# Where TensorE's weights and streamed operands lie against each other in SBUF

## The chip, the cores and the metric

The kernel runs on one core of one Trainium2 chip. The metric is the device time of one execution in microseconds (us). Three runs of the kernel before took 1624.79, 1626.24 and 1630.22 us; their median is 1626.24 us. In this text "place" is an offset along the free dimension of SBUF, the same in all 128 partitions, and "pace" is the time from the start of one matmul to the start of the next.

## The reference

Two models run one after the other on 256 tokens of width 1024, in float32. The first has two layers of: a gated feed-forward, a mixer with three branches (neighbourhood attention, gated linear attention, latent attention), and another gated feed-forward. The second has two hybrid layers and a final norm. Cut to what carries the work:

```python
def swiglu(h, w1, w3, w2):
    return (jax.nn.silu(h @ w1) * (h @ w3)) @ w2
...
    for l in range(DEPTH):                      # first model, 2 layers
        x = x + 0.5 * swiglu(rms_norm(x, ffn1_norm[l]), ffn1_w1[l], ffn1_w3[l], ffn1_w2[l])
        h = rms_norm(x, mix_norm[l])
        z = h @ w_in[l]                         # 1024 x 6752
        ...                                     # three branches on parts of z
        mixed = (gt[:, :, 0] * (y_na @ w_br_na[l])
                 + gt[:, :, 1] * (y_gla @ w_br_gla[l])
                 + gt[:, :, 2] * (y_mla @ w_br_mla[l]))
        x = x + mixed @ w_out[l]
        x = x + 0.5 * swiglu(rms_norm(x, ffn2_norm[l]), ffn2_w1[l], ffn2_w3[l], ffn2_w2[l])
...
    for l in range(DEPTH):                      # second model, 2 hybrid layers
        x = hybrid_layer(x, ...)                # x @ w_in, attention, convolution, mixed @ w_out
    return rms_norm_2(x, final_g)
```

The feed-forward width is 2816. Nearly all of the arithmetic is products of 256 tokens with weight matrices that are read once from HBM.

## The kernel before

The activations lie transposed, features on the partitions and 256 tokens along the free dimension. Every weight matrix is cut into slabs of 128 partitions by up to 1024 columns. The list of slabs is written in `emit` (`ffn_slabs`, `group`, `G`, `B`, `A`, lines 1711 to 1762), and the kernel takes them in that order.

One slab goes through three steps. `fetch` (L311) starts its DMA on SyncE's queue into one of five `raw` tiles. `convert` (L326) splits it into two float32r tiles: ScalarE writes the rounded part `H` (L337), VectorE writes the rest `L` = raw - H (L341). There are three `H` and three `L` buffers. `take` (called from `col`, `group` and others) hands the pair to TensorE and starts the fetch and conversion of a later slab. The activations are split in the same way into a high and a low part (`xh`, `xl`; `gh`, `gl` in the feed-forward; `yh`, `yl` and `mh`, `ml` in the mixers), so that each product is three matmuls: high by high, high by low, low by high.

Slabs are used in two ways.

- Loaded as weights (`mm3`, L430 to 433, called from `col`, `out_proj` and the second half of `ffn`): 128 columns of `H` or `L` are loaded into the array, and 256 tokens of the activation stream past. Three matmuls for each 128 columns, 24 for a full slab. L431 loads `H` and streams the high activations, L432 loads `H` and streams the low ones, L433 loads `L` and streams the high ones. All four feed-forwards work in this way: 44 slabs of 24 matmuls and 24 slabs of 21 or 24 each, 1584 matmuls; 6336 in the four.
- Streamed (`group`, L506 to 508, and L855 to 857 for the latent attention's second projection): 128 tokens of the activation are loaded as weights, and up to 512 columns of `H` or `L` stream past.

While one matmul streams, the weights of the next are loaded: the profile has LDWEIGHTS on a line of its own (PEld) beside the matmuls (PE).

Where a slab lies in its buffer comes from the table `PLACES`. A buffer is 1024 + 120 columns long, and slab number n uses the pair `PLACES[n % 320]`, the first for `H`, the second for `L`, in columns of 4 bytes. In the built program the streamed activations (`xh`, `xl`, `gh`, `gl`, `yh`, `yl`, `mh`, `ml`) begin 128 bytes past a multiple of 512, and every 256-token part of them too. The three `H` buffers begin 320, 288 and 256 bytes past a multiple of 512, the three `L` buffers 224, 192 and 160. So the distance of a loaded slab from the operand that streams past it, taken modulo 512 bytes, is worked out from its number; the buffers are used in the order first, third, second. In this kernel that distance differs from slab to slab.

The vector engines' work for the branches, the norms and the gates is spread over `tick` calls between matmuls.

Of the kernel before, what the change touches and what calls it, by code (L numbers as in the profile page):

```python
# [10 lines left out]
F32R = mybir.dt.float32r  # L11
# [6 lines left out]
P = 128  # L18
# [5 lines left out]
W2CUT = ((0, 7), (7, 7), (14, 8))  # L24
EPS = 1e-6
NEG = -1e30
SKEW = 120


def places():  # L30

    c = [[(16 * ((5 * i + 3 * j) % 8), 16 * j) for j in range(8)] for i in range(8)]
    c = [c[i][(j + i) % 8] for j in range(8) for i in range(8)]
    f = [(8 * a, 8 * b) for a in range(16) for b in range(16) if a % 2 or b % 2]
    return c + [f[(i * 77) % len(f)] for i in range(len(f))] + c[::-1]


PLACES = places()
BIG = 3e38
UNITS = "a0 a1 a2 a3 f0 b0 f1 b1 b2 b3".split()  # L40

# [3 lines left out]
class Pack:  # L45
# [5 lines left out]
    def add(self, name, a):  # L51
        a = np.asarray(a, np.float32).reshape(P, -1)
        self.at[name] = (self.n, self.n + a.shape[1])
        self.parts.append(a)
        self.n += a.shape[1]
# [78 lines left out]
def lay(I):  # L134
    I = {k: np.asarray(v) for k, v in I.items()}
    A = {}
    A["x"] = I["x"][0].T.reshape(KD, P, T).transpose(1, 0, 2)
    f13, f2 = [], []
    for l in range(2):
        for f in ("ffn1", "ffn2"):  # L140
# [3 lines left out]
            f2.append(w.transpose(2, 1, 0, 3).reshape(KD, P, FF))  # L144
    A["f13"], A["f2"] = np.stack(f13), np.stack(f2)

# [15 lines left out]
    for l in range(2):  # L162
# [36 lines left out]
        rpb.append(tz.transpose(1, 0, 2))  # L199
    A["mA"], A["mM"], A["uq"], A["ukv"] = np.stack(mA), np.stack(mM), np.stack(uq), np.stack(ukv)  # L200
    A["mG"], A["mB"], A["mO"], A["p1"] = np.stack(mG), np.stack(mB), np.stack(mO), np.stack(p1)
    A["up"], A["rpb"] = np.stack(up), np.stack(rpb)
    A["_p1"] = p.at
# [65 lines left out]
class Kernel:  # L269
# [41 lines left out]
    def fetch(s, between=(None,)):  # L311

        if s.pos == len(s.slabs):
            return
        src, cols, gain = s.slabs[s.pos]
        s.pos += 1
        raw = s.wp.tile([P, 1024], F32, tag="raw", name="raw", bufs=5)
        w = cols // len(between)
        for j, f in enumerate(between):
            a = slice(j * w, (j + 1) * w)  # L320
            s.nc.sync.dma_start(raw[:, a], src[:, a])
            if f:
                f()
        s.loaded.append((raw, cols, gain))

    def convert(s, n=1):  # L326

        if not s.loaded:
            return
        raw, cols, gain = s.loaded.pop(0)  # L330
        H, L = (s.wp.tile([P, 1024 + SKEW], F32R, tag=n, name=n, bufs=3)[:, o:o + 1024] for n, o in zip("HL", PLACES[s.nslab % len(PLACES)]))
        s.nslab += 1
        gs = gain() if gain else [None] * n
        w = cols // len(gs)

        def high(g, a):
            s.A.activation(H[:, a], raw[:, a], AF.Copy, **({} if g is None else {"scale": g}))  # L337

        def low(g, a):
            if g is None:  # L340
                s.V.tensor_tensor(L[:, a], raw[:, a], H[:, a].bitcast(F32), OP.subtract)  # L341
            else:
                s.V.scalar_tensor_tensor(L[:, a], raw[:, a], g, H[:, a].bitcast(F32), OP.mult, OP.subtract)

        parts = [(g, slice(j * w, (j + 1) * w)) for j, g in enumerate(gs)]
        if n > 1:
            s.todo += [lambda f=f, p=p: f(*p) for p in parts for f in (high, low)]
        else:
            s.todo += [lambda f=f: [f(*p) for p in parts] for f in (high, low)]
        s.ready.append((H, L))  # L350
# [1308 lines left out]
def setup(s):  # L1659
    nc, i = s.nc, s.i  # L1660
    s.xT = s.C("xT", [P, KD, T])
    s.xh, s.xl = s.C("xh", [P, KD, T], F32R), s.C("xl", [P, KD, T], F32R)
    s.ident = s.C("ident", [P, P])
    make_identity(nc, s.ident)
    s.ones = s.C("ones", [P, P])
    nc.gpsimd.memset(s.ones, 1.0)
    s.one = s.ones[:, :1]
    s.mhalf = s.C("mhalf", [P, 16])
    nc.gpsimd.memset(s.mhalf, -0.5)
    s.A.activation(s.W("ms", [P, 2]), s.mhalf[:, :2], AF.Silu)  # L1670
# [19 lines left out]
def setup_2(s):  # L1690

    s.ypad, s.hTd = cut(s.zero[:, :572], 2), s.zero[:, 572:].rearrange("p (c g h n) -> p c g h n", c=2, g=2, h=4)
    s.nc.gpsimd.memset(s.zero, 0.0)


def emit(tc, i, out, names):
    with ExitStack() as es:
        es.enter_context(tc.manual_schedule())
        s = Kernel(es, tc, i, names)
        prm = [[None, None], [None, None]]  # L1700

        def col(b, l, n):
            a, e = names["_p%d" % (b + 1)][n]
            return prm[b][l][:, a:e]

        def load(b, l, q=s.nc.gpsimd):
            n = "p%d" % (b + 1)
            prm[b][l] = s.W("prm", [P, max(i["p1"].shape[2], i["p2"].shape[2])])[:, :i[n].shape[2]]
            q.dma_start(prm[b][l], i[n][l])

        slabs = []
        add = lambda src, cols, gain=None: slabs.append((src, cols, gain))

        def ffn_slabs(j):
            for f in range(2 * NF):
                add(i["f13"][j, f], 1024)
            for m in range(KD):
                for k, n in W2CUT:
                    add(i["f2"][j, m][:, k * P:(k + n) * P], n * P)

        for l in range(2):
            ffn_slabs(2 * l)
            group = lambda g: [add(i["mA"][l, g, h], 1024) for h in range(4)]
            gain = lambda n, l=l: (lambda: [col(0, l, n)[:, k:k + 1] for k in range(2)])
            group(0)
            add(i["mM"][l], 1024)
            group(3)
            add(i["uq"][l][:, :512], 512, gain("cq"))
            add(i["uq"][l][:, 512:], 1024, gain("cq"))
            for k in range(2):  # L1730
                add(i["ukv"][l][:, k * 1024:(k + 1) * 1024], 1024, gain("ckv"))
            for g in (1, 4, 2, 5, 6):
                group(g)
            for b in range(3):
                G = lambda h: [add(i["mG"][l, (2, 0, 1)[b], 4 * h + j], 1024) for j in range(4)]
                for h in range(2):
                    G(h)
                    for j in range(2):
                        add(i["mB"][l, b, 2 * h + j], 1024, (lambda: [s.hg]) if b == 2 else None)
            for h in range(2):  # L1740
                for j in range(4):
                    add(i["mO"][l, h, j], 1024)
            ffn_slabs(2 * l + 1)
        for l in range(2):
            B = lambda a, b: [add(i["hB"][l, j], 1024) for j in range(a, b)]
            B(6, 10)
            B(0, 2)
            for j in range(4):
                add(i["hA4"][l, j], 568)
            A = lambda g: [add(i["hA"][l, g, j], 1024) for j in range(4)]  # L1750
            A(1)
            B(2, 6)
            B(12, 14)
            A(0)
            B(10, 12)
            B(14, 16)
            B(16, 18)
            add(i["pw"][l], 512)
            for h in range(2):
                for j in range(4):  # L1760
                    add(i["hO"][l, h, j], 1024)
        s.stream(slabs)

        setup(s)
        s.start(lambda: col(0, 0, "g_ffn1"), lambda: load(0, 0, s.nc.sync))
        late = setup_late(s)
        next(late)
        s.spawn(late, 8)
        for l in range(2):
            s.p1 = lambda n: col(0, l, n)  # L1770
            s.hg = s.W("hg", [P, 1])
            s.V.tensor_scalar(s.hg, s.p1("gla"), 0.5, None, OP.mult)
            s.ffn(lambda m: s.xn(m, s.p1("g_mix")), *((6, False) if l == 0 else ()))
            s.mix(l, lambda m: s.xn(m, s.p1("g_ffn2")))
            nb, nl = (0, 1) if l == 0 else (1, 0)
            if nb:
                setup_2(s)
            load(nb, nl)
            s.ffn(lambda m: s.xn(m, col(nb, nl, "g" if nb else "g_ffn1")))
        for l in range(2):  # L1780
            s.p2 = lambda n: col(1, l, n)
            if l == 0:
                load(1, 1)
            s.hybrid(l, (lambda m: s.xn(m, col(1, 1, "g"))) if l == 0 else s.last)
        s.final(out)
# [24 lines left out]
```

## Time and profile before

| | us |
|---|---|
| median of three runs | 1626.24 |
| lowest, highest | 1624.79, 1630.22 |
| the profiled execution | 1627.97 |
| its span, first to last instruction | 1626.2 |
| PE busy | 1598.5 (98%) |
| PEld busy | 1494.1 (92%) |
| DVE busy | 1115.1 (69%) |
| ACT busy | 863.2 (53%) |
[...]

PE is TensorE's matmuls, PEld its weight loads, DVE is VectorE, ACT is ScalarE. [...] The pace is read from the starts.

### The profile page before, as it was taken

How to read it: one execution, taken by the hardware profiler on the slowest of the kernel's cores; microseconds unless marked ns; L12 is line 12 of the kernel's file. 1: busy time of each engine (PE TensorE's matmuls, PEld its weight loads, DVE VectorE, ACT ScalarE, POOL GpSimd, SP SyncE). 2: the span in 40 equal slices, each digit the busy share in tenths (PEclk: the TensorE clock that was granted, in tenths of full speed). 3: DMA queues.
4: the chain of work that ended last, by engine and by line, in shares of the span. 5: the costliest groups of instructions: out<-in, count | busy, mean ns of one | idle time of the engine just before them, and what ended most of it. 6: DMA issues, size and time to landing. Idle time of an engine off the chain costs nothing.

```text
span 1626.2 us, 30862 instructions
## 1 busy us (share of the span) xinstructions
PE 1598.5 (98%) x12446; PEld 1494.1 (92%) x12446; DVE 1115.1 (69%) x1841; ACT 863.2 (53%) x1455; POOL 246.6 (15%) x334
## 2 busy tenths in 40 slices
PE   8999999999999999999999999999999999998998
PEld 8999988799999999999998879999999988887887
DVE  6666667667676665666656776777666578868885
ACT  5444466654445444444446765444444435864684
POOL 2000232311030001100013231103000221113101
PEclk9999999999999999999999999999999999999999
DMA  6555554433555556655565453455555655336431
GB/s 246 189 184 178 195 189 143 163 113 136 185 172 182 188 177 189 197 183 180 179 201 174 143 168 117 143 183 171 193 182 181 191 193 203 114 113 212 172 111 53
DMA packets 78127, 275.92 MB, mean 170 GB/s; under 512 B 8768, under 2 KB 8912, under 8 KB 77984
## 3 DMA queue, kind: packets, MB, share of 16 engines
q1 hardware_dynamic: 76320, 267.47, 48.9%
q0 software_dynamic: 1520, 6.22, 1.2%
q8 instruction: 97, 1.59, 0.4%
q14 instruction: 46, 0.38, 0.1%
q10 hardware_dynamic: 144, 0.26, 0.0%
HBM read 272.87 MB, written 1.05 MB: 168 GB/s over the span
## 4 chain that ended last, share of the span: by engine, by line
PE 92%; DVE 3%; POOL 2%; ACT 1%; issue 1%; DMA 1%; SPq 0%; POOLq 0%; DVEq 0%; ACTq 0%
PE pd L431 21%; PE pd L433 21%; PE pd L432 21%; PE pd L506 4%; PE pd L507 4%; PE pd L508 4%; PE pa L432 2%; PE pa L431 2%; PE pa L433 2%; PE pa L699 2%; PE pa L448 1%; POOL ss L466 1%; DVE L L341 1%; DVE xl L455 1%; PE pa L678 1%
## 5 line engine op out<-in xcount | busy, mean ns | idle before, releaser
L341 DVE TENSOR_TENSOR L<-raw,H 128x1024 fp32r<-128x1024 f32 (+2 forms) x490 | 593.8, 1217 | 241.2 <-ACT H L337 238.5
L337 ACT ACTIVATE H<-raw 128x1024 fp32r<-128x1024 f32 (+2 forms) x490 | 503.3, 1029 | 300.8 <-PE pd L432 115.0
L431 PE MATMUL pd<-xh,H 128*128 128x256 f32 x1840 | 523.1, 284 | 0.0
L433 PE MATMUL pd<-xh,L 128*128 128x256 f32 x1840 | 517.2, 281 | 0.8 <-DVE L L341 0.8
L432 PE MATMUL pd<-xl,H 128*128 128x256 f32 x1840 | 517.2, 281 | 0.3 <-DVE xl L455 0.2
L431 PEld LDWEIGHTS pd<-xh,H 128*128 128x128 f32 x1840 | 347.3, 189 | 7.2 <-issue 6.4
L432 PEld LDWEIGHTS pd<-xl,H 128*128 128x128 f32 x1840 | 347.3, 189 | 1.0 <-DVE xl L455 0.7
L433 PEld LDWEIGHTS pd<-xh,L 128*128 128x128 f32 x1840 | 347.1, 189 | 1.0 <-DVE L L341 1.0
L432 PE MATMUL pd<-gl,H 128*128 128x256 f32 x704 | 197.7, 281 | 0.0
L433 PE MATMUL pd<-gh,L 128*128 128x256 f32 x704 | 197.5, 281 | 0.0
L431 PE MATMUL pd<-gh,H 128*128 128x256 f32 x704 | 197.5, 281 | 0.0
L590 ACT ACTIVATE u<-t 128x256 f32<-128x256 f32 x88 | 36.8, 418 | 186.9 <-DVE t L588 186.9
L433 PEld LDWEIGHTS pd<-gh,L 128*128 128x128 f32 x704 | 132.7, 189 | 0.0
L431 PEld LDWEIGHTS pd<-gh,H 128*128 128x128 f32 x704 | 132.5, 188 | 0.0
L432 PEld LDWEIGHTS pd<-gl,H 128*128 128x128 f32 x704 | 132.4, 188 | 0.0
L506 PE MATMUL pd<-H,xh 128*128 128x512 f32 (+1 forms) x320 | 129.8, 406 | 0.0
L507 PE MATMUL pd<-L,xh 128*128 128x512 f32 (+1 forms) x320 | 123.7, 387 | 2.4 <-DVE L L341 2.4
L508 PE MATMUL pd<-H,xl 128*128 128x512 f32 (+1 forms) x320 | 123.2, 385 | 0.0
L462 POOL TENSOR_TENSOR ss<-xT 128x256 f32<-128x256 f32 x9 | 5.5, 613 | 666.9 <-DVE xT L609 501.2
L454 ACT ACTIVATE xh<-xT,prm 128x256 fp32r<-128x256 f32 x64 | 30.7, 505 | 112.0 <-DVE xT L609 90.9
L431 PE MATMUL pa<-xh,H 128*128 128x256 f32 x256 | 74.2, 290 | 6.2 <-ACT H L337 6.2
L506 PEld LDWEIGHTS pd<-H,xh 128*128 128x128 f32 x320 | 60.4, 189 | 17.7 <-issue 6.2
(416 smaller groups left out, 2713.7 us busy)
## 6 DMA issues: line engine op xcount, KB each, us to landing
raw<-in_f SPq DMA_DIRECT2D x206, 512.0 KB, 3.6
raw<-in_f SPq DMA_DIRECT2D x64, 448.0 KB, 3.4
raw<-in_mA SPq DMA_DIRECT2D x56, 512.0 KB, 3.3
raw<-in_mG SPq DMA_DIRECT2D x48, 512.0 KB, 3.2
raw<-in_hB SPq DMA_DIRECT2D x36, 512.0 KB, 4.2
raw<-in_mB SPq DMA_DIRECT2D x24, 512.0 KB, 3.3
raw<-in_mO SPq DMA_DIRECT2D x16, 512.0 KB, 3.3
raw<-in_hA SPq DMA_DIRECT2D x16, 512.0 KB, 3.3
```

The source lines that it names most:

```text
L337: s.A.activation(H[:, a], raw[:, a], AF.Copy, **({} if g is None else {"scale": g}))
L341: s.V.tensor_tensor(L[:, a], raw[:, a], H[:, a].bitcast(F32), OP.subtract)
L431: s.T.matmul(out, lh, rh, start=start, stop=False)
L432: s.T.matmul(out, lh, rl, start=False, stop=False)
L433: s.T.matmul(out, ll, rh, start=False, stop=stop)
L448: s.T.transpose(pt[:, tok(c)], src[:, tok(c)], s.ident)
L454: s.A.activation(s.xh[:, k], s.xT[:, k], AF.Copy, scale=g[:, k:k + 1])
L506: s.T.matmul(o, s.xh[:, k, t], H[:, c], start=(k == 0), stop=False)
L507: s.T.matmul(o, s.xh[:, k, t], L[:, c], start=False, stop=False)
L508: s.T.matmul(o, s.xl[:, k, t], H[:, c], start=False, stop=(k == KD - 1))
L590: s.A.activation(u, t, AF.Silu)
L699: s.T.matmul(out[tb][h], q[r, tok(tb)], k[r, :ws[tb]], start=start or tb == 0, stop=start)
```

## The change

The table of places is replaced by two short ones. `LOAD` has three pairs, used in turn, for slabs that are loaded as weights; `STREAM` has one, (0, 0), for slabs that are streamed. Each entry of the slab list carries the table it uses. The buffers grow from 1024 + 120 to 1024 + 128 columns, and a tile `pad` of 80 columns that nothing reads is added after `xl`. With it the three `H` and three `L` buffers all begin 128 bytes past a multiple of 512, as the activations do. So a loaded slab lies at these distances from the operand that streams past it, modulo 512 bytes: `H` at 64 and `L` at 448, then 320 and 448, then 64 and 320. A streamed slab lies at distance 0 from the activations loaded against it. Three buffers and three pairs go round together. There are two exceptions. The four slabs of `hA4` in each hybrid layer hold two parts of 284 columns, and the second begins 1136 bytes on, so it is not level. And the activations for the slab `pw` lie elsewhere: there the distances are 192 for `H` and 64 for `L`.

`pad` also moves the constants behind it (the identity used by transposes, `kT`, `rT`, `zero` and others) by 320 bytes. On all five engines the instructions and their order stay what they were, and so do shapes, DMAs and waits.

```diff
-SKEW = 120
-
-
-def places():
-
-    c = [[(16 * ((5 * i + 3 * j) % 8), 16 * j) for j in range(8)] for i in range(8)]
-    c = [c[i][(j + i) % 8] for j in range(8) for i in range(8)]
-    f = [(8 * a, 8 * b) for a in range(16) for b in range(16) if a % 2 or b % 2]
-    return c + [f[(i * 77) % len(f)] for i in range(len(f))] + c[::-1]
-
-
-PLACES = places()
+SPARE = 128
+
+
+STREAM, LOAD = ((0, 0),), ((16, 112), (80, 112), (16, 80))
...
-        src, cols, gain = s.slabs[s.pos]
+        src, cols, gain, places = s.slabs[s.pos]
...
-        s.loaded.append((raw, cols, gain))
+        s.loaded.append((raw, cols, gain, places))
...
-        raw, cols, gain = s.loaded.pop(0)
-        H, L = (s.wp.tile([P, 1024 + SKEW], F32R, tag=n, name=n, bufs=3)[:, o:o + 1024] for n, o in zip("HL", PLACES[s.nslab % len(PLACES)]))
+        raw, cols, gain, places = s.loaded.pop(0)
+        H, L = (s.wp.tile([P, 1024 + SPARE], F32R, tag=n, name=n, bufs=3)[:, o:o + 1024] for n, o in zip("HL", places[s.nslab % len(places)]))
...
     s.xh, s.xl = s.C("xh", [P, KD, T], F32R), s.C("xl", [P, KD, T], F32R)
+    s.C("pad", [P, 80])
...
-        add = lambda src, cols, gain=None: slabs.append((src, cols, gain))
+        add = lambda src, cols, gain=None, places=LOAD: slabs.append((src, cols, gain, places))
...
-            group = lambda g: [add(i["mA"][l, g, h], 1024) for h in range(4)]
+            group = lambda g: [add(i["mA"][l, g, h], 1024, None, STREAM) for h in range(4)]
...
-                add(i["hA4"][l, j], 568)
-            A = lambda g: [add(i["hA"][l, g, j], 1024) for j in range(4)]
+                add(i["hA4"][l, j], 568, None, STREAM)
+            A = lambda g: [add(i["hA"][l, g, j], 1024, None, STREAM) for j in range(4)]
```

The slabs of `uq` and `ukv` get `STREAM` in the same way.

## Rows read from the trace of the kernel before

**Rows 1.** The page's busy time by engine: us (share of the span) x instructions.

```profile
PE 1598.5 (98%) x12446; PEld 1494.1 (92%) x12446; DVE 1115.1 (69%) x1841; ACT 863.2 (53%) x1455; POOL 246.6 (15%) x334
```

**Rows 2.** The page's chain that ended last: shares of the span by engine and line.

```profile
PE 92%; DVE 3%; POOL 2%; ACT 1%; issue 1%; DMA 1%; SPq 0%; POOLq 0%; DVEq 0%; ACTq 0%
PE pd L431 21%; PE pd L433 21%; PE pd L432 21%; PE pd L506 4%; PE pd L507 4%; PE pd L508 4%; PE pa L432 2%; PE pa L431 2%; PE pa L433 2%; PE pa L699 2%; PE pa L448 1%; POOL ss L466 1%; DVE L L341 1%; DVE xl L455 1%; PE pa L678 1%
```

**Rows 3.** Waits of PE, two longest: us in total, times, longest.

```profile
PE pa L431 <- ACT H L337: 6.2, 1, 6.2
PE pa L1378 <- DMA raw<-in_cw: 2.8, 2, 1.9
```

**Rows 4.** The page's costliest groups: xcount | busy us, mean ns of one | idle before.

```profile
L341 DVE TENSOR_TENSOR L<-raw,H 128x1024 fp32r<-128x1024 f32 (+2 forms) x490 | 593.8, 1217 | 241.2 <-ACT H L337 238.5
...
L432 PE MATMUL pd<-xl,H 128*128 128x256 f32 x1840 | 517.2, 281 | 0.3 <-DVE xl L455 0.2
...
L432 PE MATMUL pd<-gl,H 128*128 128x256 f32 x704 | 197.7, 281 | 0.0
...
L508 PE MATMUL pd<-H,xl 128*128 128x512 f32 (+1 forms) x320 | 123.2, 385 | 0.0
```

**Rows 5.** Stretches: us, PE, PEld, DVE, ACT, POOL busy (x), PEclk, DMA share, GB/s.

```profile
475.00:845.00 370.00, 369.12 (x3130) 368.91 (x3129) 234.07 (x320) 174.15 (x241) 27.24 (x34) 1.00 0.57 185
...
1121.00:1323.00 202.00, 201.11 (x1703) 200.90 (x1702) 128.31 (x177) 95.01 (x131) 20.67 (x28) 1.00 0.56 184
...
1480.00:1490.00 10.00, 8.79 (x70) 8.56 (x69) 9.86 (x19) 3.15 (x6) 0.00 (x0) 1.00 0.47 159
1490.00:1500.00 10.00, 9.11 (x59) 5.16 (x58) 9.65 (x23) 3.50 (x6) 4.03 (x8) 1.00 0.89 319
```

**Rows 6.** PE in order of time, slabs 212 to 215: start us, us, instruction.

```profile
657.62 0.28 PE L431 MATMUL pd<-gh,H 128*128 128x256 f32 x1
...
660.00 0.28 PE L431 MATMUL pa<-xh,H 128*128 128x256 f32 x1
...
665.10 0.28 PE L431 MATMUL pa<-xh,H 128*128 128x256 f32 x1
```

**Rows 7.** Groups of the stretch 657.6 to 665.1, one of three alike.

```profile
L432 PE MATMUL pa<-xl,H 128*128 128x256 f32 x15 | 4.1, 276 | 0.0
```

**Rows 8.** PE in order of time, slabs 164, 165 and the first half of 166.

```profile
527.06 0.28 PE L431 MATMUL pd<-xh,H 128*128 128x256 f32 x1
...
532.72 0.28 PE L431 MATMUL pd<-xh,H 128*128 128x256 f32 x1
...
533.07 0.28 PE L431 MATMUL pd<-xh,H 128*128 128x256 f32 x1
...
533.98 0.28 PE L433 MATMUL pd<-xh,L 128*128 128x256 f32 x1
```

**Rows 9.** PE in order of time, slab 186: its first matmul and the next slab's.

```profile
589.38 0.28 PE L431 MATMUL pd<-xh,H 128*128 128x256 f32 x1
...
592.25 0.28 PE L431 MATMUL pd<-xh,H 128*128 128x256 f32 x1
```

**Rows 10.** PE in order of time, slab 116, which begins after two small matmuls.

```profile
382.98 0.38 PE L431 MATMUL pd<-xh,H 128*128 128x256 f32 x1
383.20 0.28 PE L432 MATMUL pd<-xl,H 128*128 128x256 f32 x1
...
384.15 0.28 PE L431 MATMUL pd<-xh,H 128*128 128x256 f32 x1
...
384.49 0.28 PE L431 MATMUL pd<-xh,H 128*128 128x256 f32 x1
```

**Rows 11.** PE in order of time, two streamed slabs.

```profile
281.73 0.39 PE L506 MATMUL pd<-H,xh 128*128 128x512 f32 x1
...
282.87 0.39 PE L508 MATMUL pd<-H,xl 128*128 128x512 f32 x1
...
1345.03 0.39 PE L507 MATMUL pd<-L,xh 128*128 128x512 f32 x1
...
1345.96 0.40 PE L508 MATMUL pd<-H,xl 128*128 128x512 f32 x1
```

More of the change, by code (lines that the diff above doesn't have):

```diff
@@ L1727, in emit @@
             group(3)
-            add(i["uq"][l][:, :512], 512, gain("cq"))
-            add(i["uq"][l][:, 512:], 1024, gain("cq"))
+            add(i["uq"][l][:, :512], 512, gain("cq"), STREAM)
+            add(i["uq"][l][:, 512:], 1024, gain("cq"), STREAM)
             for k in range(2):
-                add(i["ukv"][l][:, k * 1024:(k + 1) * 1024], 1024, gain("ckv"))
+                add(i["ukv"][l][:, k * 1024:(k + 1) * 1024], 1024, gain("ckv"), STREAM)
             for g in (1, 4, 2, 5, 6):
```

## The prediction

> **What bounds the kernel now.** I read the page's busy times first: PE is busy for 98% of the span [rows 1]. The chain that ended last says the same of the end: 92% of it is PE, and L431, L432 and L433, the three matmuls of a slab loaded as weights, hold some 21% each [rows 2]. The waits of PE come next: the longest in total is 6.2 us, once, at the start, and the next 2.8 us [rows 3]. So neither a DMA nor another engine paces this kernel: the stream of matmuls does, and the question is only how fast one follows another.
>
> The duration column cannot answer that, since rows overlap. A stretch can: from 475 to 845 us, two feed-forwards and nothing else, PE starts 3130 matmuls in 370.00 us, 118.2 ns each; from 1121 to 1323 us it is 202/1703 = 118.6 ns [rows 5]. The list in order of time, summed over the 9,572 matmuls of L431 to L433 with no pause behind them (starts less than 140 ns apart), gives 118.1 ns as well.
>
> That mean hides two steady paces. Slabs 212 to 215 run from 657.62 to 665.10 us: 22 triples, 66 matmuls, 7.48/66 = 113.3 ns [rows 6]. Their rows also last 276 ns [rows 7], where the mean over the kernel is 281 [rows 4]: a second witness that needs no subtraction. Slabs 164 and 165 need 5.66 us for 48 matmuls, 117.9 ns, and the pattern repeats evenly [rows 8]. Slab 186 takes 2.87 us for 24, 119.6 ns [rows 9]. In all of these the granted clock is the full one, no engine is waited for, and the matmul and the load have the same shape. What differs is the place.
>
> **Which places run fast.** From the table of places, the buffer starts and the slab's number I worked out the distance of H and L from the streamed operand for all 416 slabs loaded as weights, and put the pace of each beside it. Example: slab 213 has the pair (96, 24) in the first buffers, so H starts at 320 + 384 = 704, which is 192, and 64 behind the stream's 128; L at 224 + 96 = 320, 192 behind. In 25 slabs both distances are odd multiples of 64. Of these, 17 settle at 113 ns and 8 stay near 118. Of the other 391 not one settles at 113. So the condition is necessary for the fast pace in this trace, and it is sufficient in part.
>
> The 25 sort further, by the distances modulo 256. H at 64 and L at 192: 7 of 7 settle at 113 (slabs 116, 117, 166, 212, 213, 466, 495). Both at 64: 4 of 7. Both at 192: 2 of 5; H 192 and L 64: 4 of 6. Slabs 164 and 165 have both at 192 and keep the slow pace that they inherit; slab 166, with H at 64 and L at 448, leaves it within three matmuls: from 533.07 to 533.98 eight starts take 0.91 us, 113.8 ns [rows 8]. And a slab that inherits the fast pace with odd distances keeps it, as 213, 214 and 215 do after 212, with no slow start between them [rows 6].
>
> The change gives every slab loaded as weights odd distances. Its first two pairs, (64, 448) and (320, 448), are of the class with 7 of 7; the third, (64, 320), is both at 64, and its one example in this trace (slab 416) settles too. If a pause puts PE in the slow pace at a slab of the third pair, the next slab brings it out.
>
> **The change part by part.**
>
> Feed-forwards: 6336 matmuls at 118.2 [rows 5], to be 113.4 (113.3 and a few restarts): 6336 x 4.8 = 30 us, with little beside them to wait for. Slabs come every 24 x 113.4 = 2.72 us then, and VectorE needs 1.22 us for L [rows 4] and is busy for 234/370 = 63% of such a stretch [rows 5], 66% after; the DMAs' share of 0.57 becomes 0.59. Both hold.
>
> Mixers and hybrid layers: L431 to L433 have 9768 matmuls in all, so 3432 here. At 4.7 each this is 16 us, less what restarts cost. After a pause the first matmuls are slow whatever the place: in slab 116, of the best class, eight starts take 0.95 us (119 ns) and only then does it go at 0.34/3 = 113 [rows 10]; the others of its kind took 2 to 10. The list shows some 150 pauses in these stages. Taking seven slow matmuls after each and counting only what is left leaves 12 us of the 16.
>
> Waits that come late: where PE waits for work that does not get shorter, an earlier arrival is lost. VectorE is busy for 9.86 and 9.65 of 10 us at 1480 to 1500 us, the start of a hybrid layer, where PE falls to 8.79 and 9.11 [rows 5]; PE starts about 170 matmuls in the 20 us before such a place, so up to 170 x 4.7 = 0.8 us goes there, twice. Chains at the ends of the stages lose less each. I take 3 us lost, between 0 and 8 (half of the 16).
>
> Streamed slabs: 1056 matmuls. Before, starts of the 512-column ones lie 231.9 ns apart in the mean of the list. One slab happened to be level in both parts: 0.93 us for four starts, 232.5 ns [rows 11]. The fastest stretch ran at 1.14/5 = 228 ns [rows 11], and the slowest slabs near 236. So the change is worth +0.6 ns x 936 = +0.5 us, with -4 and +4 us as bounds; I take +0.5, the level slab's own.
>
> The moved constants: transposes and small products read from another place. They stream 128 columns at most for the greater part, fill under a tenth of the span between them, and no view here sets their pace against place; I take 0, within 2 us either way.
>
> Sum: -30 - 12 + 3 + 0.5 = -38.5 us. The profiled execution took 1627.97 us with a span of 1626.2; it lies 1.7 above the median of the runs. 1627.97 - 38.5 - 1.7 gives 1588 us.
>
> [...] The rows show one load and one matmul at full clock going at 113.3, 117.9 or 119.6 ns by place alone [rows 6, 8, 9]. [...]
>
> **The rivals.**
>
> A, the forecast: the fast pace holds nearly everywhere. 1588, 1579 to 1597 with the bounds above. Chance 0.80.
>
> B, the slow pace is kept in about half of the slabs: pauses start it and the rotation does not end it, or a step from one pair to the next brings it back. For it: 8 of the 25 slabs, and no two slabs of the new pairs stand side by side in this trace. Against it: 7 of 7. The gain on loaded slabs halves: 1626 - 20 = 1606. Chance 0.07.
>
> C, PE arrives early and waits: conversions or DMAs become the bound in the mixers and hybrid layers, whose whole 12 us is lost, and a quarter of the feed-forwards' 30 too. For it: VectorE at 98% in the stretch above [rows 5]. Against it: 63% in the feed-forwards, and PE's short waits [rows 3]. 1626 - 22 = 1604. Chance 0.05.
>
> [...] Chance 0.04.
>
> E, slower: the quiet distance is not the one I computed but one of absolute places, and one of the three fixed pairs is a bad one. A bad slab ran at 123.8 ns in the worst case of the list; a third of 9768 matmuls at that pace, the others as before, is 3256 x 5.7 = 18.6 us more: 1645. It decides from a mean above 118.1. Against it: the fast slabs sit in all three buffers at nine or more places. Chance 0.04.
>
> **How the numbers follow.** A difference under 0.3% (5 us) counts as none here. A, B and C are faster: 0.92. D is the same: 0.04; E slower: 0.04. The range takes in A, C and B and the unknown bounds: 1577 to 1610.
>
> **What would show it.** The groups of L431 to L433 should last 276 to 277 ns, not 281. The two-feed-forward stretch should hold its 3130 matmuls in 355 us. In the list, slabs should follow each other at 113 without a step. L508 should stay near 385 ns. PE's waits should stay under 25 us in all. Rows at 117.9 in long runs speak for B, new waits of PE on L337 or L341 for C, and a mean at 118 with odd distances would refute me.

## The result, and the profile after

Four runs of the changed kernel took 1581.15 to 1583.11 us, median 1581.89; the kernel before took 1627.1 us in the median of four runs (the three shown, and one beside the new kernel). The ratio of the runs is 0.9722, with a 95% interval from 0.9703 to 0.974. The forecast was 1588 us, in a range from 1577 to 1610. The profiled execution took 1581.15 us with a span of 1579.4. The mean granted clock of TensorE was 0.998 in it, and 0.997 in the profiled execution of before.

The engines' line of the page, for the kernel after; the one of before is in [rows 1]:

```profile
PE 1550.6 (98%) x12446; PEld 1449.1 (92%) x12446; DVE 1113.3 (70%) x1841; ACT 861.9 (55%) x1455; POOL 249.8 (16%) x334
```

PE's busy time fell by 47.9 us with the same number of instructions. VectorE, ScalarE and GpSimd do what they did, within 4 us each. PE is still the bound, at the same 98%. Its rows overlap, some 277 ns long with 113.7 from start to start in the loaded slabs, so this share does not tell the pace.

The groups of the page answer to [rows 4]. The lines are 8 lower in the changed file: L424 is what was L432, L500 what was L508.

```profile
L424 PE MATMUL pd<-xl,H 128*128 128x256 f32 x1840 | 509.0, 277 | 0.4 <-DVE xl L447 0.2
...
L424 PE MATMUL pd<-gl,H 128*128 128x256 f32 x704 | 194.3, 276 | 0.0
...
L500 PE MATMUL pd<-H,xl 128*128 128x512 f32 (+1 forms) x320 | 121.9, 381 | 0.0
```

A loaded slab's matmul lasts 276 to 277 ns where it lasted 281, and the streamed one 381 where it lasted 385. The 276 is the duration that [rows 7] showed for one stretch of the kernel before: what was the exception is now the rule.

The next rows are the start of a hybrid layer, as in the last two of [rows 5], and the stretch that holds the same two feed-forwards as its first. The columns are those of [rows 5].

```profile
1436.00:1446.00 10.00, 8.62 (x63) 8.09 (x62) 9.85 (x21) 3.99 (x6) 0.93 (x4) 1.00 0.52 170
1446.00:1456.00 10.00, 9.17 (x59) 5.28 (x57) 8.60 (x21) 3.48 (x6) 3.16 (x5) 1.00 0.93 327
461.00:816.50 355.50, 354.56 (x3127) 354.36 (x3127) 232.81 (x319) 173.84 (x241) 26.24 (x33) 1.00 0.59 192
```

The feed-forwards go at 355.5/3127 = 113.7 ns a matmul, against 118.2. The DMAs' share is 0.59, as worked out ahead, and PE waits for no DMA in this stretch. In the hybrid layer VectorE is still full for 10 us (9.85), and PE falls back there as before (8.62 and 9.17 of 10 us).

The two longest waits of PE, beside [rows 3]:

```profile
PE pa L423 <- ACT H L329: 5.9, 1, 5.9
PE pa L1370 <- DMA raw<-in_cw: 3.2, 2, 2.3
```

Over the whole list of PE's waits the sum goes from 20.8 to 21.6 us. The 16 pauses of over 700 ns between two matmuls' starts take 18.7 us before and 19.8 after; three of the four pauses in the hybrid layers' starts grew by 0.85 us together.

Summed from start to start, the 46.8 us by which the span is shorter divide so: the 9768 matmuls of loaded slabs take 1138.4 us where they took 1181.6 (-43.2); the 1056 of streamed slabs take 246.0 where they took 249.0 (-2.9, of which the 512-column ones without a pause go from 231.9 to 228.5 ns); all other matmuls 182.3 where they took 182.6; the last 0.3 lies before the first matmul and behind the last. Of the loaded ones without a pause, 118.1 ns has become 113.7.

What is left of the slow pace is, for the greater part, the restart after a pause or after other matmuls, at all three pairs: 200 starts of 116 ns or more are in the 141 slabs at (64, 448), 180 in the 143 at (320, 448), and 241 in the 140 at (64, 320). (These counts, here and below, leave out the two `pw` slabs; ten slabs that are used in two pieces count twice, which makes 424.) Slow for long are mostly slabs of the third pair, as the prediction expected: ten of them have more than 12 slow starts, six to their end and four up to a break in their middle. Of the other two pairs three have so many, each broken in its middle, so that it restarts twice. One of the ten, PE in order of time, begins after four small matmuls:

```profile
643.28 0.50 PE L468 MATMUL pa<-ones,ss 128*128 128x1 f32 x4
643.64 0.36 PE L423 MATMUL pa<-xh,H 128*128 128x256 f32 x1
643.84 0.28 PE L424 MATMUL pa<-xl,H 128*128 128x256 f32 x1
...
646.67 0.28 PE L424 MATMUL pa<-xl,H 128*128 128x256 f32 x1
...
646.91 0.28 PE L423 MATMUL pa<-xh,H 128*128 128x256 f32 x1
...
647.83 0.28 PE L425 MATMUL pa<-xh,L 128*128 128x256 f32 x1
```

From 643.84 to 646.67 us 24 starts take 117.9 ns each. From 646.91 to 647.83, in the next slab, at (64, 448), eight take 0.92 us, 115 ns: the slow pace ends within it.

### The profile page after: what moved, and what is told of

The parts are those of the page before. It is cut to its first block, busy times and chain, and to the rows that moved or that the text cites. A ratio compares the mean times of both kernels' runs of the same rounds, so it can differ in the third digit from the quotient of the medians.

```text
span 1579.4 us, 30862 instructions
## 1 busy us (share of the span) xinstructions
PE 1550.6 (98%) x12446; PEld 1449.1 (92%) x12446; DVE 1113.3 (70%) x1841; ACT 861.9 (55%) x1455; POOL 249.8 (16%) x334
## 4 chain that ended last, share of the span: by engine, by line
PE 92%; DVE 3%; POOL 2%; ACT 1%; DMA 1%; issue 1%; SPq 0%; POOLq 0%; DVEq 0%; ACTq 0%
PE pd L423 21%; PE pd L424 20%; PE pd L425 20%; PE pd L498 4%; PE pd L499 4%; PE pd L500 4%; PE pa L424 2%; PE pa L423 2%; PE pa L425 2%; PE pa L691 2%; PE pa L440 1%; POOL ss L458 1%; DVE L L333 1%; PE pa L670 1%; POOL sq L457 1%
## 5 line engine op out<-in xcount | busy, mean ns | idle before, releaser
L423 PE MATMUL pd<-xh,H 128*128 128x256 f32 x1840 | 515.0, 280 | 0.0
L425 PE MATMUL pd<-xh,L 128*128 128x256 f32 x1840 | 509.0, 277 | 0.9 <-DVE L L333 0.8
L424 PE MATMUL pd<-xl,H 128*128 128x256 f32 x1840 | 509.0, 277 | 0.4 <-DVE xl L447 0.2
L424 PEld LDWEIGHTS pd<-xl,H 128*128 128x128 f32 x1840 | 345.8, 188 | 1.0 <-DVE xl L447 0.8
L425 PE MATMUL pd<-gh,L 128*128 128x256 f32 x704 | 194.3, 276 | 0.0
L423 PE MATMUL pd<-gh,H 128*128 128x256 f32 x704 | 194.3, 276 | 0.0
L424 PE MATMUL pd<-gl,H 128*128 128x256 f32 x704 | 194.3, 276 | 0.0
L424 PEld LDWEIGHTS pd<-gl,H 128*128 128x128 f32 x704 | 132.2, 188 | 0.0
L500 PE MATMUL pd<-H,xl 128*128 128x512 f32 (+1 forms) x320 | 121.9, 381 | 0.0
```

The costliest lines, as they stand in the source:

```text
L423: s.T.matmul(out, lh, rh, start=start, stop=False)
L424: s.T.matmul(out, lh, rl, start=False, stop=False)
L425: s.T.matmul(out, ll, rh, start=False, stop=stop)
L500: s.T.matmul(o, s.xl[:, k, t], H[:, c], start=False, stop=(k == KD - 1))
```

## The experiments

The theory: TensorE streams one operand while the next weights are loaded (in the changed kernel its matmuls are busy for 98% of the span and its weight loads for 92%), and what decides the pace is the distance between the two in SBUF modulo 256 bytes; two steady paces exist, and the class of the pair says whether PE leaves the slow one. Rivals: the absolute place of a slab, the alternation of pairs, the moved constants, or the phase in which a slab is met.

**The distance alone, within one run.** Because `gh`, `yh` and `mh` lie behind the slab buffers and `xh` before them, a smaller pad moves all slabs against `xh` and none against `gh`.

```diff
-    s.C("pad", [P, 80])
+    s.C("pad", [P, 72])
```

> The pad is 72 columns instead of 80, so all six slab buffers move by 32 bytes, and so do gh, gl, yh, yl, mh and ml, which are allocated behind them; xh and xl stay. Slabs against which xh or xl stream (6288 of the 9768 matmuls) are now at distances 32, 288 and 416 from the stream, slabs against which gh, yh or mh stream keep 64, 320 and 448; the streamed slabs lie 32 bytes off level. Theory (the distance between loaded weights and streamed operand decides): matmuls on xh and xl go back to about 118 ns, those on gh, yh and mh stay at 113.3 to 114; the streamed ones go from 227 back to about 232 ns. Time 1582 + 6288 x 4.6 ns + 936 x 4 ns = about 1615 us. Rival (it is the absolute place of the slab, or the turn of three pairs): both kinds of matmul behave alike, either all near 113.5 (1582 us) or all near 118 (1625 us).

Measured: 1613.05 us, ratio to before 0.9916 (0.9896 to 0.9935); 1615 was worked out. Groups of this kernel:

```profile
L424 PE MATMUL pd<-xl,H 128*128 128x256 f32 x1840 | 516.8, 281 | 0.4 <-DVE xl L447 0.2
...
L424 PE MATMUL pd<-gl,H 128*128 128x256 f32 x704 | 194.4, 276 | 0.0
```

Same line, same buffers, same run: 281 ns against `xl`, 276 against `gl`. From start to start it is 118.3 ns on `xh` and `xl`, 113.4 on `gh` and `gl`, 114.4 and 113.4 on the mixers' operands, and streamed slabs fall back to 232.6. The instructions and their order are the same as in the changed kernel, and so is the turn of the pairs; only slabs whose distance moved went back to the slow pace. The absolute place of a slab is excluded, and the phase theory too: the distance decides. (The smaller pad also moves the constants, by 32 bytes; the next experiment shows nothing that their place is worth.)

**The constants.**

```diff
-    s.C("pad", [P, 80])
...
     s.kcz = s.C("kcz", [P, 2, 64])
+    s.C("pad", [P, 80])
```

> The pad is allocated behind the last constant instead of behind xl: the slab buffers and all distances are those of the changed kernel, while the identity, kT, rT, zero and the other constants go back to where they were before the change. Theory: the constants' places are worth nothing measurable, 1582 us within 2 us; transposes keep their time. Rival (part of the gain that the prediction did not forecast comes from the moved constants): 3 to 6 us slower than the changed kernel, with slower transposes and scores.

Measured: 1582.22 us, ratio 0.9724 (0.9709 to 0.9738). All matmuls that are not of slabs take 182.6 us, as before the change. The largest group of transposes, in the changed kernel:

```profile
L440 PE MATMUL pa<-ident,z 128*128 128x128 f32 x80 | 11.1, 274 | 0.0
```

The same group in the experiment, where the identity lies 320 bytes lower:

```profile
L440 PE MATMUL pa<-ident,z 128*128 128x128 f32 x80 | 11.1, 274 | 0.0
```

The moved constants are worth nothing that these runs show.

**One pair, no alternation.**

```diff
-STREAM, LOAD = ((0, 0),), ((16, 112), (80, 112), (16, 80))
+STREAM, LOAD = ((0, 0),), ((16, 112),)
```

> Every loaded slab uses one pair, (16, 112), distances 64 and 448; nothing alternates. Theory (what counts is the class of the pair, H at 64 and L at 192 modulo 256, which always leaves the slow pace): as fast as the changed kernel or up to 2 us faster, 1580 to 1582 us, with no slab that keeps 118 ns to its end. Rival (alternation is what ends the slow pace): long runs of 118 ns and 1590 us or more.

Measured: 1582.31 us, ratio 0.9731 (0.9715 to 0.9747), as fast as the three pairs. Three slabs are slow in more than 12 starts, against 13 with the three pairs; each of the three is broken in its middle and restarts twice, and none is slow to its end. Loaded matmuls without a pause take 113.62 ns. Alternation is not needed for this class.

**The third pair alone, and a pair at 192.** Two kernels, each with one pair of equal distances modulo 256:

```diff
-STREAM, LOAD = ((0, 0),), ((16, 112), (80, 112), (16, 80))
+STREAM, LOAD = ((0, 0),), ((16, 80),)
```

> Every loaded slab uses the third pair, (16, 80), distances 64 and 320: both odd multiples of 64, equal modulo 256. Theory (such a pair is free of stalls but keeps the slow pace when a pause has put PE in it): inside one run both paces, whole runs of slabs at 117.8 ns after a pause and at 113.3 before one; between 1590 and 1624 us. Rival (any odd distances will do, and the third pair's slow slabs in the changed kernel come from what precedes them): 1582 us, slow slabs only directly after a pause.

Measured: 1604.99 us, ratio 0.9879 (0.9861 to 0.9897). Two stretches of feed-forward in this one run, columns as in [rows 5]:

```profile
30.00:185.00 155.00, 155.00 (x1370) 155.00 (x1369) 101.45 (x139) 75.14 (x106) 8.14 (x11) 1.00 0.60 192
480.00:640.00 160.00, 160.00 (x1361) 160.00 (x1360) 99.91 (x136) 74.27 (x103) 9.42 (x13) 1.00 0.58 188
```

Both have the same instructions, the same places and the full clock: 155/1370 = 113.1 ns and 160/1361 = 117.6 ns. In the list the pace changes only where a pause or other matmuls stand between, and holds from one such place to the next. Cut at every start of 140 ns or more and at every other matmul, the loaded slabs of this run make 60 unbroken stretches of 12 starts or more. From the tenth start on 37 of them go at 113 to 114 ns and 23 at 117.7 to 119; none changes over, the longest slow one in 1547 starts. Of the 60 such stretches of the changed kernel 58 end at the fast pace, and of the 60 with the first pair alone all do. So the slow pace is a state of the stream, not a property of a place; a pair of this class keeps either, and a pair of the first class leaves the slow one.

```diff
-STREAM, LOAD = ((0, 0),), ((16, 112), (80, 112), (16, 80))
+STREAM, LOAD = ((0, 0),), ((112, 48),)
```

> Every loaded slab uses (112, 48), distances 448 and 192: odd, equal modulo 256, both 192 there. Theory: as with the third pair alone, slow runs that last from a pause to the next event that ends them, 1590 to 1624 us. Rival (odd distances suffice): 1582 us.

Measured: 1621.24 us, ratio 0.9973 (0.9962 to 0.9985). The groups of loaded slabs:

```profile
L424 PE MATMUL pd<-xl,H 128*128 128x256 f32 x1840 | 514.6, 280 | 0.3 <-DVE xl L447 0.2
...
L424 PE MATMUL pd<-gl,H 128*128 128x256 f32 x704 | 196.9, 280 | 0.0
```

Here 9461 of 9557 starts are slow, mean 117.74 ns, and 405 of the 424 slabs have more than 12 of them. The time lies within what was expected, near its upper end: I expected both paces in long runs, and the fast one is there only in pieces, for 42 starts near the kernel's beginning and then for some ten starts at a time. Odd distances alone gave nearly nothing here.

**The fourth class.**

```diff
-STREAM, LOAD = ((0, 0),), ((16, 112), (80, 112), (16, 80))
+STREAM, LOAD = ((0, 0),), ((112, 16),)
```

> Every loaded slab uses (112, 16), distances 448 and 64: odd, unequal modulo 256, but H at 192 and L at 64. The pw slab, the only one at such distances in the changed kernel, ran at 118 to 124 ns to its end after its pause. Theory (this class keeps a slow pattern once a pause has started it, and keeps the fast one otherwise): long runs at 118 to 119 ns after pauses, others at 113; 1590 to 1628 us. Rival (what matters is only that H and L differ by 128 modulo 256): 1582 us, as for the first two pairs.

Measured: 1615.9 us, ratio 0.9936 (0.9893 to 0.9978). Feed-forward stretches of this run:

```profile
40.00:185.00 145.00, 145.00 (x1222) 145.00 (x1221) 90.28 (x122) 66.71 (x93) 6.61 (x9) 1.00 0.56 183
480.00:640.00 160.00, 160.00 (x1414) 160.00 (x1413) 104.77 (x144) 79.84 (x113) 8.15 (x11) 1.00 0.58 192
```

It goes at 118.7 ns in the first and 113.2 in the second. The class with H at 192 and L at 64 is the mirror of the good one, and it keeps both paces: 42 of its 60 unbroken stretches are slow from the tenth start on. That H and L differ by 128 is not enough: H must be the one at 64.

**Only the good class.**

```diff
-STREAM, LOAD = ((0, 0),), ((16, 112), (80, 112), (16, 80))
+STREAM, LOAD = ((0, 0),), ((16, 112), (80, 112), (80, 48))
```

> The third pair is replaced by (80, 48), distances 320 and 192, so that all three pairs have H at 64 and L at 192 modulo 256. Theory: the ten slabs that kept 118 ns to their end in the changed kernel leave it after at most ten matmuls: 10 x 14 x 4.5 ns = 0.6 us, and as much again in shorter restarts; 1580.5 to 1582 us, against 1581.9. Rival (the third pair's slow slabs are no matter of its class): the same number of them as before, at other places.

Measured: 1584.16 us (1580.66 to 1585.71 in five runs), ratio 0.9753 (0.974 to 0.9766). In the profile the ten slow slabs at the third pair are gone, and slow starts fall from 621 to 452, 169 x 4.5 ns = 0.8 us; the profiled span is 1578.9 against 1579.4. The runs do not show so little, and their median lies 2 us on the other side. The mechanism is as expected; a faster kernel is not shown, and none of these experiments beats the changed kernel.

**How exact the distance must be.**

```diff
-STREAM, LOAD = ((0, 0),), ((16, 112), (80, 112), (16, 80))
+OFF = (-8, -4, -2, -1, 1, 2, 4, 8)
+STREAM, LOAD = ((0, 0),), tuple(p for o in OFF for p in ((16, 112), (16 + o, 112 + o)))
```

> Every second loaded slab uses (16, 112), distances 64 and 448; those between use the same pair moved by -32, -16, -8, -4, 4, 8, 16 and 32 bytes, one after the other. It asks how exact the distance has to be. If only whole multiples of 64 are quiet, every moved slab runs at 117 to 120 ns and the time is about 1582 + 0.5 x 9768 x 5 ns = 1606 us. If what counts is a line or bank of 16 or 32 bytes, those moved by less than that run at 113 as well and the time is 1588 to 1595 us.

Measured once: 1610.2 us, near the 1606 of the first case. What follows compares slabs within this one run. Starts without a pause, by the slab's distance of H (L moved with it):

| H at | 32 | 48 | 56 | 60 | 64 | 68 | 72 | 80 | 96 |
|---|---|---|---|---|---|---|---|---|---|
| mean ns | 118.3 | 119.7 | 118.2 | 119.1 | 114.9 | 118.2 | 119.8 | 118.0 | 117.8 |
| share at 114 or less | 3% | 0% | 4% | 1% | 69% | 0% | 26% | 12% | 3% |

One float, 4 bytes, off the mark is as bad as 32. The 64 column has the good slabs that lie between moved ones: they have to come out of the slow pace each time, and 69% of their starts are fast. At 72 a quarter of the starts are as fast, but the others so slow that the mean is the worst of the row. No line or bank of 16 or 32 bytes fits this: the slabs moved by 4 to 16 bytes take 118.0 to 119.8 ns in the mean.

**The streamed slabs, each way.**

```diff
-STREAM, LOAD = ((0, 0),), ((16, 112), (80, 112), (16, 80))
+STREAM, LOAD = ((16, 112), (80, 112), (16, 80)), ((16, 112), (80, 112), (16, 80))
```

> Streamed slabs use the three pairs of the loaded ones instead of lying level. Theory (level is what brings 512-column matmuls from 231.9 to 227 ns): they go to 231 to 233 ns, 936 x 5 ns = 4 to 5 us slower than the changed kernel, about 1586 us; the loaded slabs' pace is unchanged. Rival (the streamed slabs gained because the slabs around them run fast, or from the even buffers): 227 ns and 1582 us again.

Measured: 1586.32 us, ratio 0.9751 (0.9732 to 0.9771). Streamed 512-column matmuls take 230.3 ns without a pause, loaded ones 113.7 as in the changed kernel. The pace is under what was expected (231 to 233 ns): (230.3 - 228.5) x 842 = 1.5 us for those without a pause; the profiled span is 3.8 us longer, 2.9 of it at the streamed slabs with their pauses. So of the 3.4 ns that streamed matmuls gained, level brings 1.8; the other 1.6 came in this run without it.

The other way round, level streams beside the long table of before (its function `places` is taken over as it stood):

```diff
-STREAM, LOAD = ((0, 0),), ((16, 112), (80, 112), (16, 80))
+STREAM, LOAD = ((0, 0),), places()
```

> The streamed slabs lie level as in the changed kernel; the loaded ones take their places from the long table of before. Theory (the two parts of the change act apart): streamed 512-column matmuls at 227 to 228.5 ns, loaded ones at 118.1 ns; 1626 - 3 = about 1623 us. Rival (streamed matmuls gained because their neighbours ran fast): 231.9 ns and 1626 us.

Measured: 1622.5 us, ratio 0.9966 (0.9955 to 0.9977). Streamed matmuls 228.6 ns, loaded ones 118.0. The two halves of the change act apart. PE in order of time shows how a level stretch starts in this kernel, here after eight transposes:

```profile
218.46 0.48 PE L506 MATMUL pd<-H,xh 128*128 128x512 f32 x1
218.78 0.39 PE L507 MATMUL pd<-L,xh 128*128 128x512 f32 x1
...
219.94 0.39 PE L506 MATMUL pd<-H,xh 128*128 128x512 f32 x1
...
224.92 0.39 PE L507 MATMUL pd<-L,xh 128*128 128x512 f32 x1
```

The first five starts, 218.78 to 219.94, take 232 ns each; the 22 from 219.94 to 224.92 take 4.98 us, 226.4 each. In the changed kernel it is the same on average: in its 64 level stretches the first three starts without a pause take 232.0 ns, those from the tenth on 226.9. Level has an entry of three to six slow starts and then a steady pace of its own.

## Why the prediction was right

The bound, the mechanism and the sign were right. PE's pace was the bound and still is. The 113.3 ns found in a few slabs of the trace of before is what nearly all loaded slabs now run at: a sum of -42 us for the two loaded terms, -43.2 measured. The second, inherited pace exists, and the sort by class held: the two pairs with 7 of 7 leave it, and the third pair can keep it (ten slabs in the changed kernel; 244 of 424 slabs with more than 12 slow starts when that pair is alone). In the changed kernel the next slab brings PE out again, as the rows from 646.91 us show. Rival B, slow pace in half of the slabs, is thus a real outcome of pairs that the change does not use or uses only between others. Rival D, for which place is not the cause and what looks like it is the phase in which a slab was met, falls with the 32-byte shift: place does change the time, 118.3 against 113.4 ns in one run. What makes the distance count, no run here shows. Rival E is excluded by the measured time and by the same run, rival C by PE's waits, 21.6 us in all.

One reading was off by a number. The stretch named slabs 212 to 215 [rows 6] belongs to slabs 212 to 214: 213 and 214 are used in two pieces each. Slab 215 begins after four small matmuls, lies at (448, 160), is none of the 25, and goes at 117.9 ns. That an inherited fast pace is kept rests on 213 and 214, which show it.

The forecast was 6 us too high, and two terms of the sum were mis-sized. The span got 46.8 us shorter, not 38.5; of the 8.3 between them, 3.4 are the streamed slabs, 3 the late waits, 1.2 the loaded slabs, and 0.7 all the rest. (8.3 is more than 6 because it compares the two profiled executions: the one before lay 1.7 us above its median, which the forecast took off, the one after 0.7 below.) That the loaded slabs come out so close is in part luck: the feed-forwards gained 29.1 us where 30 was forecast, the mixers and hybrid layers 14.1 where 12 was. Seven slow starts after each of 150 pauses were allowed for there, 1050; the trace has 550 of 116 ns or more.

"Streamed slabs" was taken at +0.5 us and measured -2.9, and so the sign that L508 stays near 385 ns failed: the group lasts 381. The step that failed was to read the price of level from one slab [rows 11]: its four starts, between pauses, were the entry that the last rows above show, 232 ns, not the steady pace of 227 behind it, which no slab of the kernel before ran long enough to show. The bound of the term was -4, so the range held it.

"Waits that come late" was taken at 3 us lost. The 16 longer pauses grew by 1.1 us, which the sums by kind of matmul hold already, so that nothing was lost beside these sums. At the hybrid starts the mechanism was as described, VectorE full and PE waiting longer, but three pauses grew by 0.85 us in all and the fourth shrank by 0.07, where up to 0.8 was worked out for each of two places; the other twelve pauses grew by 0.3 in all.

## What to carry to other kernels

Where PE is the bound and matmuls follow without waits, compare start-to-start times of equal matmuls before changing anything else: two values of it in one trace are a finding, as 113.3 and 117.9 ns were here. In this kernel the stream had two steady states at the same placement (113.1 and 117.6 ns a matmul with the third pair alone), so a placement is judged by whether it leaves the slow one after a pause, not by its best stretch. Level brought the 512-column matmuls from 231.9 to 228.5 ns and the 256-column ones from about 118 to between 119 and 120, so the distance is tried for each shape. And a rate read from a few starts behind a pause was that of the entry here, 232 ns where 226.4 to 227 followed: take it from the middle of a long stretch, or keep the bound wide.

## What the runs showed of the hardware

- A float32r matmul of 256 columns with 128 columns of weights loaded beside it goes at 113.3 ns at best and at 117.8 in a second steady state. Where the distances are not odd multiples of 64 bytes it goes at about 118 on average and up to 123.8 in one slab (the kernel before). Level, 512 columns go at 226.4 to 227 ns behind the entry, against 231.9 in the mean of the kernel before.
- The distance counts to 4 bytes: 60 and 68 are as slow as 32 (119.1, 118.2 and 118.3 ns).
- A single program with one placement, the third pair, ran one feed-forward stretch at 113.1 and another at 117.6 ns a matmul; only pauses and other matmuls moved it between the two.
- With H and L both at 192 modulo 256 the fast pace was rarely entered: 96 of 9557 starts are under 116 ns, and the mean is 117.74. It can be kept there all the same: slab 214 of the kernel before, at such distances, follows a fast slab and goes at 113.4.
- For the same level placement 256 streamed columns take 119 to 120 ns in 22 of 24 starts (the slabs of the latent attention with that width), against about 118 in the kernel before, so the level that is faster for 512 columns is slower for 256.

What makes the two steady states, and why the order of H and L matters, is not settled: the runs tell which placements leave the slow one, not what holds it.
